# Filler projections: weights loaded and split half a group ahead, splits issued behind the newest probabilities' parts, in pieces of 512 columns

## The chip, the cores and the metric

The kernel runs on one core of one Trainium2 chip. The metric is the device time of one execution in microseconds (us); the time before is the median of three runs. The engines are TensorE (PE in the profile, its weight loads PEld), VectorE (DVE), ScalarE (ACT), GpSimd (POOL) and SyncE (SP), which here only issues DMAs. Each engine works through its own list of instructions in order; semaphores join the lists.

## The reference

One inference step of a layer with d_model 1024, for 256 context tokens and 1024 latent tokens. Both kinds of tokens go through the same normalised input, two token mixers side by side, a gated merge, one output projection, and a squared-ReLU MLP:

```python
h = rms_norm(x, norm_mix_w) * (1.0 + sc1) + sh1
z = h @ w_in                       # 1024 x 5376
hq, hf_f, hf_b, hi, hg, aq, ak, av, gl = jnp.split(z, _split_points(), axis=-1)
...                                # q, k normed, rotated; latent also sees 512 cached keys
o_a = block_attention(q, k_all, v_all)                      # 8 heads, 2 kv heads, 64 wide
o_h, s_final = hgrn_branch(hq, hf_f, hf_b, hi, hg, ...)     # scan in both directions
g = jax.nn.sigmoid(gl).reshape(b, l, 2, 1024)
merged = g[:, :, 0] * (o_h @ w_ho) + g[:, :, 1] * (o_a @ w_ao)
x = x + g1 * (merged @ w_out)
h = rms_norm(x, norm_ffn_w) * (1.0 + sc2) + sh2
x = x + g2 * (jnp.square(jax.nn.relu(h @ w_ff1)) @ w_ff2)
```

The shifts, scales and gates (sh1, sc1, g1, sh2, sc2, g2) are columns of silu(c) @ w_ada + b_ada, the adaLN product. All of it is float32. The 5376 columns of w_in are: hq, hf_f, hf_b, hi, hg with 512 each (for the scan), the queries, keys and values of the attention, and gl with 2048 (the merge gates).

## The kernel before

**Products.** A float32 product is made of three matmuls of a rounded type: each operand is split into a high part (rounded) and a low part (what is left), and high x high, high x low and low x high are added. The helper `split` does this to a piece of weights in SBUF: ACT copies it to the high part with rounding (L277), and DVE subtracts that from the raw piece to give the low part (L278). The matmuls of `mm3` are L308, L309 and L310.

**Stages.** The kernel goes through: normalisation and the projection of the attention's q, k, v (to about 150 us), the attention (to about 710 us), the scan of the HGRN branch (to about 1010 us), the merge and output projection, and the MLP. Attention and scan leave gaps on TensorE where a softmax or a recurrence isn't ready, so their matmuls are interleaved with those of projections that need nothing from them, the *filler*.

**The filler.** A group of the filler is 256 columns of w_in, applied to all 1280 tokens. During the attention run ten groups, five for each half of the scan's channels: hq, hf_f, hf_b as *channel groups* (`z_ch`: channels on the partitions, two halves of 128 columns after one another, 24 steps of three matmuls each), hi and hg as *token groups* (`z_tok`: tokens on the partitions, L325 to L327, 80 steps). During the scan run eight groups of gl, all channel groups. The class `Filler` advances such a generator by a given share of time between the matmuls of the attention or the scan. `with_ada` strings groups together and puts one block of 256 columns of the adaLN product behind each: a load of w_ada, 32 matmuls (L178), and a late part (a transposition L184 and a column sum `adas` on DVE, L186), which is called at the seventh step of the next group.

**The weights of a group.** `wraw` allots one of two buffers and issues the DMA of 1 MB (1024 x 256) on SP; the loads of w_in and w_ada take turns in them. `w_oc` (a half of a channel group) and `w_kh` (a half of a token group's rows) take two of six buffers `wsp`, a high and a low, and call `split` once for 1024 columns. All this stands in the program where the group, or its second half, begins.

**The attention.** A unit is one head and 256 queries. For the latent tokens its keys are three blocks of 512, and the unit goes through six *parts*: `trans` transposes two 128-key slices of the normalised probabilities `pexp` for both row blocks into one PSUM bank (L738), ACT takes the high part `pTh` of it (L741), DVE the low part `pTl` (L742), and `value` multiplies both with the values (L753 with `pTh`, L754 with `pTl`). Meanwhile the next unit's softmax runs: scores (L697) into three banks, maxima `mx` (DVE, L698), their negated maximum `ngm` (L702), three exponentials `pexp` for each row block (ACT, L708), the reciprocal sum `rs` (L711, L712), and the multiplication with it (L716), in turn on POOL and DVE.

**What sets the order.** TensorE's list is written out by the program (events of the units, merged by time, with filler between). The lists of ACT, DVE, POOL and SP are set by the framework's list scheduler: it simulates the program with costs of its own and issues on each engine, as buffers come free, what is ready, lower program order first. `tc.high_priority(offset=n)` makes it treat instructions as n earlier. Splits therefore go to the lists as soon as it believes the raw weights landed and the buffers free.

Of the kernel before, what the change touches and what calls it, by code (L numbers as in the profile page):

```python
# [44 lines left out]
def build(ctx, tc, I, O, C):  # L45
# [27 lines left out]
    def PS(tag, shape=(P, 512)):  # L73
        tag = "g" if tag == "p" else tag
        return ps.tile(list(shape), F32, tag=tag, name="ps_" + tag, bufs=PSB[tag])
# [30 lines left out]
    def f32(ap):  # L106
        return ap.bitcast(F32)
# [168 lines left out]
    def split(hi, lo, raw):  # L276
        s_.activation(hi, raw, AF.Copy)  # L277
        return v.tensor_tensor(lo, raw, f32(hi), op=ALU.subtract)  # L278
# [11 lines left out]
    def w_oc(raw, half, kcs=KC):  # L290

        hi, lo = wsp((P, kcs, P)), wsp((P, kcs, P))
        last_split[0] = split(hi, lo, raw[:, :, half * P:(half + 1) * P])
        return hi, lo

    def w_kh(raw, half):
        hi, lo = wsp((P, 4, 256)), wsp((P, 4, 256))
        split(hi, lo, raw[:, half * 4:half * 4 + 4, :])
        return hi, lo

    def mm3(out, wt, kcs, mov, first=True, last=True, mid=None):
# [27 lines left out]
                        consume(pr, po)  # L329
                    yield 0.327  # L330

    def z_ch(c0, consume, begun=None):

        raw, wt = begun or (wraw(I["w_in"], KC, c0), None)
        for half in range(2):
            if half or wt is None:
                wt = w_oc(raw, half)
            for t, (t0, n, cond) in enumerate(TT):
                po = PS("g")
                for k in range(KC):  # L340
                    mm3(po[:, 0:n], (wt[0][:, k:k + 1], wt[1][:, k:k + 1]), 1, hT[t][k:k + 1], k == 0, k == KC - 1)
                    if k == KC - 1:
                        consume(half, t, po[:, 0:n])
                    yield n * 0.00128

    def run(gen):
        for _ in gen:
# [313 lines left out]
    class Unit:  # L661
# [71 lines left out]
        def trans(self, p2):  # L733
            pt = PS("t", (P, 2, 256))
            for a in range(2):
                i, kg, b = self.kt[2 * p2 + a]
                for j in range(2):
                    pe.transpose(pt[:, a, j * P:(j + 1) * P], self.Ps[j][i][:, b * P:(b + 1) * P], ident)  # L738
            hi = S((P, 2, 256), F32R, name="pTh")
            lo = S((P, 2, 256), F32R, name="pTl")  # L740
            s_.activation(hi, pt, AF.Copy)  # L741
            v.tensor_tensor(lo, pt, f32(hi), op=ALU.subtract)  # L742
            self.pt[p2] = hi, lo

        def value(self, p2):
# [334 lines left out]
        return f  # L1080

    def zh(c):
        return (z_ch(HQ + 256 * c, hq_consume(c)), z_ch(HF + 256 * c, hf_consume(0, c)),
                z_ch(HF + 512 + 256 * c, hf_consume(1, c)), z_tok(HI + 256 * c, hi_consume(c)),
                z_tok(HG + 256 * c, hg_consume(c)))

    todo = []

    def with_ada(gens, b0):

        for i, gen in enumerate(gens):
            for j, x in enumerate(gen):
                if j == 6 and todo:
                    todo.pop()()
                yield x
            if b0 + i < 16:
                raw = wraw(I["w_ada"], KC, 2 * D + (b0 + i) * 256)
                ci = 16 + 2 * (b0 + i)
                todo.append(ada_cols(PS("g"), raw, ci))
                yield 1.8  # L1100
        if todo and b0:
            todo.pop()()
# [6 lines left out]
    R = S(name="R")  # L1109
    g_.memset(R, 0.0)  # L1110
    g_.memset(R.rearrange("p (c i) -> p c i", i=32)[:, :, 0:1], 1.0)
    raw = wraw(I["w_in"], KC, GL)
    with tc.high_priority(offset=600):
        begun = [(raw, w_oc(raw, 0))] + 7 * [None]
    fg = Filler(with_ada([z_ch(GL + 256 * c, gl_consume(c), begun[c]) for c in range(8)], 10), 194.0)
    hgrn(fg, fz.rest)
    fg.rest()
    close("sl")
# [708 lines left out]
```

## Time and profile before

| | |
|---|---|
| Time, median of 3 runs | 2056.11 us (2056.02 to 2057.93) |
| Time of the profiled execution | 2055.24 us |
| Its span, first to last instruction | 2053.1 us |
| Granted TensorE clock, mean | 0.998 |
| Busy in the span: PE, PEld, DVE, ACT, POOL | 2012.3, 1736.1, 1405.3, 938.5, 546.1 us |
| Splits of weights `wsp<-wraw`: ACT, DVE (all stages) | 109.7 us, 139.9 us (110 each) |
| High and low parts of probabilities `pTh` (ACT), `pTl` (DVE) | 118.4 us, 135.9 us (200 each) |

The profile is one execution. A row of a group of instructions names line, engine, operation, output<-input tile, shape and count. A row of the timeline gives start, duration and, in brackets, for how long the engine had been idle and which work of which engine ended that. TensorE is busy 98% of the span; its idle time in the stages of the attention and the scan is the small remainder in which the change acts.

### The profile page before, as it was taken

The page shows a single profiled execution, that of the slowest core. Times are in us where ns is not written, and L with a number is a line of the kernel's source. Part 1 is how long each engine was busy: PE and PEld are TensorE (multiplying, and loading weights), DVE is VectorE, ACT ScalarE, POOL GpSimd, SP SyncE. Part 2 cuts the span into 40 slices and gives each one's busy share as a digit, 9 for nine tenths or more (in the row PEclk, how much of TensorE's full clock was granted, in tenths as well). Part 3 has the DMA queues.
Part 4 walks back from the last instruction along what each step waited for, and adds up shares of the span by engine and source line. Part 5 has one row for each costly group of instructions (what it writes and reads, how often), then busy time and mean ns, then how long its engine had stood idle before and what let it go on. Part 6 is the DMA issues. An engine that isn't in the chain of part 4 may idle for free.

```text
span 2053.1 us, 33691 instructions
## 1 busy us (share of the span) xinstructions
PE 2012.3 (98%) x12470; PEld 1736.1 (85%) x12470; DVE 1405.3 (68%) x2655; ACT 938.5 (46%) x1906; POOL 546.1 (27%) x566
## 2 busy tenths in 40 slices
PE   6899999999999999999999999999999999999998
PEld 5798889988889988888888889998888888888886
DVE  4876776777776788779254634886666666577686
ACT  4735555555555423332321335655455544333443
POOL 1473333333332265545112101222122110000130
PEclk9999999999999999999999999999999999999999
DMA  9453220322211455455544533864444489455764
GB/s 309 150 187 97 78 77 27 108 86 78 78 45 65 132 175 167 153 173 159 196 138 149 180 113 116 259 186 151 157 147 157 145 292 361 148 159 176 232 238 142
DMA packets 220052, 317.38 MB, mean 155 GB/s; under 512 B 18504, under 2 KB 139168, under 8 KB 219888
## 3 DMA queue, kind: packets, MB, share of 16 engines
q1 hardware_dynamic: 207216, 275.05, 41.7%
q0 software_dynamic: 12672, 40.18, 5.5%
q8 instruction: 98, 1.61, 0.3%
q14 instruction: 66, 0.54, 0.1%
HBM read 229.43 MB, written 85.74 MB: 154 GB/s over the span
## 4 chain that ended last, share of the span: by engine, by line
PE 62%; DVE 2%; issue 1%; ACT 0%; DMA 0%; POOL 0%; POOLq 0%; ACTq 0%; DVEq 0%
PE ps_g L308 5%; PE ps_g L309 5%; PE ps_g L310 5%; PE ps_g L1614 2%; PE ps_g L1616 2%; PE ps_g L1615 2%; PE ps_s L1460 2%; PE ps_s L1461 2%; PE ps_s L1459 2%; PE ps_s L1614 2%; PE ps_s L1615 2%; PE ps_s L1616 2%; PE ps_t L1614 2%; PE ps_t L1615 2%; PE ps_t L1616 2%; PE ps_s L308 2%
## 5 line engine op out<-in xcount | busy, mean ns | idle before, releaser
L308 PE MATMUL ps_g<-hs,wsp 128*128 128x512 f32 (+1 forms) x896 | 322.2, 360 | 1.1 <-DVE adas L186 1.0
L310 PE MATMUL ps_g<-hs,wsp 128*128 128x512 f32 (+1 forms) x896 | 309.3, 345 | 0.0
L309 PE MATMUL ps_g<-hs,wsp 128*128 128x512 f32 (+1 forms) x896 | 309.1, 345 | 0.0
L716 POOL TENSOR_SCALAR pexp<-pexp,rs 128x512 f32<-128x512 f32 (+1 forms) x104 | 171.5, 1655 | 364.8 <-ACT pTh L741 210.6
L277 ACT ACTIVATE wsp<-wraw 128x1024 fp32r<-128x1024 f32 x110 | 109.7, 997 | 276.6 <-PE ps_g L309 82.8
L278 DVE TENSOR_TENSOR wsp<-wraw,wsp 128x1024 fp32r<-128x1024 f32 x110 | 139.9, 1272 | 114.8 <-ACT wsp L277 114.4
L308 PEld LDWEIGHTS ps_g<-hs,wsp 128*128 128x128 f32 x896 | 169.6, 189 | 22.3 <-issue 4.6
L310 PEld LDWEIGHTS ps_g<-hs,wsp 128*128 128x128 f32 x896 | 169.3, 189 | 21.5
L309 PEld LDWEIGHTS ps_g<-hs,wsp 128*128 128x128 f32 x896 | 169.9, 190 | 14.8
L741 ACT ACTIVATE pTh<-ps_t 128x512 fp32r<-128x512 f32 x200 | 118.4, 603 | 124.5 <-PE ps_t L738 124.4
L277 ACT ACTIVATE ah<-ar 128x640 fp32r<-128x640 f32 (+1 forms) x112 | 80.9, 723 | 185.1 <-PE ps_g L1615 102.3
L698 DVE TENSOR_REDUCE mx<-ps_s 128x1 f32<-128x512 f32 (+1 forms) x208 | 137.1, 663 | 37.7 <-PE ps_s L697 36.9
L708 ACT ACTIVATE pexp<-ps_s,ngm 128x512 f32<-128x512 f32 (+1 forms) x208 | 137.4, 670 | 43.7 <-DVE ngm L702 42.9
L278 DVE TENSOR_TENSOR ah<-ar,ah 128x640 fp32r<-128x640 f32 (+1 forms) x112 | 93.1, 832 | 77.2 <-ACT ah L277 76.1
L742 DVE TENSOR_TENSOR pTl<-ps_t,pTh 128x512 fp32r<-128x512 f32 x200 | 135.9, 681 | 14.1 <-ACT pTh L741 13.9
L697 PE MATMUL ps_s<-Kl,Ql 128*128 128x512 f32 (+1 forms) x416 | 130.7, 411 | 0.7 <-ACT pexp L708 0.7
L738 PE MATMUL ps_t<-ident,pexp 128*128 128x128 f32 x800 | 120.8, 273 | 3.3 <-DVE pTl L742 1.8
L325 PE MATMUL ps_g<-wsp,hs 128*128 128x256 f32 x400 | 115.9, 290 | 0.0
L327 PE MATMUL ps_g<-wsp,hs 128*128 128x256 f32 x400 | 112.9, 282 | 0.0
L326 PE MATMUL ps_g<-wsp,hs 128*128 128x256 f32 x400 | 112.5, 281 | 0.0
L754 PE MATMUL ps_g<-pTl,Vl 128*128 128x256 f32 x400 | 105.9, 287 | 4.0 <-DVE pTl L742 4.0
L738 PEld LDWEIGHTS ps_t<-ident,pexp 128*128 128x128 f32 x800 | 93.6, 140 | 14.1 <-issue 4.0
(421 smaller groups left out, 5395.2 us busy)
## 6 DMA issues: line engine op xcount, KB each, us to landing
ar<-AF SPq DMA_DIRECT2D x112, 320.0 KB, 3.2
wraw<-in_w_ff SPq DMA_DIRECT2D x32, 1024.0 KB, 6.1
wr<-in_w_ff SPq DMA_DIRECT2D x128, 256.0 KB, 4.4
wraw<-in_w_in SPq DMA_DIRECT2D x18, 1024.0 KB, 5.7
wraw<-in_w_ada SPq DMA_DIRECT2D x16, 1024.0 KB, 5.6
AF<-a POOLq DMA_DIRECT2D x48, 256.0 KB, 2.7
AF<-t POOLq DMA_DIRECT2D x48, 256.0 KB, 2.4
wa<-in_w_ada SPq DMA_DIRECT2D x32, 256.0 KB, 5.8
```

The lines of the kernel that those rows point to most:

```text
L277: s_.activation(hi, raw, AF.Copy)
L278: return v.tensor_tensor(lo, raw, f32(hi), op=ALU.subtract)
L308: pe.matmul(out, hi[:, k, :], mh, start=(first and k == 0), stop=False)
L309: pe.matmul(out, hi[:, k, :], ml, start=False, stop=False)
L310: pe.matmul(out, lo[:, k, :], mh, start=False, stop=(last and k == kcs - 1))
L697: pe.matmul(pq[:, 0:n], self.qh[:, q0:q0 + P], K[self.g][var][self.kts[i]], start=(var == 0), stop=(var == 1))
L698: v.tensor_reduce(self.mx[j][:, i:i + 1], pq[:, 0:n], axis=AX.X, op=ALU.max)
L708: s_.activation(e[:, 0:n], self.ps.pop((j, i))[:, 0:n], AF.Exp, bias=self.mx[j], accum_out=self.sm[j][:, i:i + 1])
L716: NORM[(i + j) % len(NORM)].tensor_scalar(x, x, self.rs[j], None, op0=ALU.mult)
L738: pe.transpose(pt[:, a, j * P:(j + 1) * P], self.Ps[j][i][:, b * P:(b + 1) * P], ident)
L742: v.tensor_tensor(lo, pt, f32(hi), op=ALU.subtract)
L1614: pe.matmul(bank, ph, wh, start=first and i == 0, stop=False, **more)
```

## The change

The two generators of a channel group become one for a half (`z_half`). A class `Group` holds a group's buffer and its split halves: `load` issues the load, `part(i)` splits half i, and `stages` yields what is to be multiplied. `with_ada` now calls these ahead: at half of a channel group's first half, its second half is split; at 5% of a group's last half (or of a token group's 80 steps) the load of the next group is issued in the program, and at 50% its first half is split, for a token group behind a channel group at 75% also the second.

While a split is issued it is ordered behind the newest `pTh` (on ACT) and the newest `pTl` (on DVE) that the program had made by then (`tc.issue_after` on both), which the attention leaves in `behind`. Behind the attention, `behind` still holds the last parts, so in the scan the rule holds nothing back.

Each split is cut into pieces of 512 columns, an ACT and a DVE instruction for each: `w_oc` in four of its eight slices at a time, `w_kh` in two of four. `w_oc` also serves the output projection later, with 8 splits of 1024 columns that become 16.

```diff
     def w_oc(raw, half, kcs=KC):
         hi, lo = wsp((P, kcs, P)), wsp((P, kcs, P))
-        last_split[0] = split(hi, lo, raw[:, :, half * P:(half + 1) * P])
+        for k in range(0, kcs, 4):
+            last_split[0] = split(hi[:, k:k + 4], lo[:, k:k + 4], raw[:, k:k + 4, half * P:(half + 1) * P])
         return hi, lo
     def w_kh(raw, half):
         hi, lo = wsp((P, 4, 256)), wsp((P, 4, 256))
-        split(hi, lo, raw[:, half * 4:half * 4 + 4, :])
+        for k in range(0, 4, 2):
+            split(hi[:, k:k + 2], lo[:, k:k + 2], raw[:, half * 4 + k:half * 4 + k + 2, :])
         return hi, lo
...
+    behind = [None, None]
+    class Group:
+        def __init__(self, c0, consume, tok):
+            self.c0, self.consume, self.tok = c0, consume, tok
+            self.raw, self.w = None, [None, None]
+        def load(self):
+            if self.raw is None:
+                self.raw = wraw(I["w_in"], KC, self.c0)
+        def part(self, i):
+            if self.w[i] is not None:
+                return
+            self.load()
+            with ExitStack() as after:
+                for x in behind:
+                    if x is not None:
+                        after.enter_context(tc.issue_after(x.ins))
+                self.w[i] = (w_kh if self.tok else w_oc)(self.raw, i)
+            if i == 1:
+                self.raw = None
+        def stages(self):
+            if self.tok:
+                self.part(0)
+                self.part(1)
+                w, self.w = self.w, [0, 0]
+                yield (0, 1), 80, z_tok(self.c0, self.consume, w)
+                return
+            for half in range(2):
+                self.part(half)
+                w, self.w[half] = self.w[half], 0
+                yield (half,), 24, z_half(w, half, self.consume)
+                del w
...
-            s_.activation(hi, pt, AF.Copy)
-            v.tensor_tensor(lo, pt, f32(hi), op=ALU.subtract)
+            behind[:] = s_.activation(hi, pt, AF.Copy), v.tensor_tensor(lo, pt, f32(hi), op=ALU.subtract)
...
-    def with_ada(gens, b0):
-        for i, gen in enumerate(gens):
-            for j, x in enumerate(gen):
-                if j == 6 and todo:
-                    todo.pop()()
-                yield x
+    def with_ada(groups, b0):
+        for i, grp in enumerate(groups):
+            nxt = groups[i + 1] if i + 1 < len(groups) else None
+            for need, n, gen in grp.stages():
+                if not grp.tok and need == (0,):
+                    jobs = [(0.5, lambda: grp.part(1))]
+                elif nxt:
+                    jobs = [(0.05, nxt.load), (0.5, lambda: nxt.part(0))]
+                    if nxt.tok and not grp.tok:
+                        jobs.append((0.75, lambda: nxt.part(1)))
+                else:
+                    jobs = []
+                for j, x in enumerate(gen):
+                    if 0 in need and j == 6 and todo:
+                        todo.pop()()
+                    while jobs and j >= jobs[0][0] * n:
+                        jobs.pop(0)[1]()
+                    yield x
...
-    raw = wraw(I["w_in"], KC, GL)
+    gls = [Group(GL + 256 * c, gl_consume(c), False) for c in range(8)]
     with tc.high_priority(offset=600):
-        begun = [(raw, w_oc(raw, 0))] + 7 * [None]
+        gls[0].part(0)
```

The lists of instructions show what the scheduler makes of it. TensorE's list of matmuls is the same in both kernels. On the other engines, at three places (in the changed kernel the line numbers are some 37 higher: `pTh` and `pTl` both stand at L778, `pexp` at L745, `mx` at L735, `ngm` at L739, `ze`, the evacuation of a projection, at L878 and L879, where it was L842 and L843).

The first place is DVE in a latent unit in the middle of the attention, the one that runs around 517 us. Before:

```order
L742 TENSOR_TENSOR pTl<-ps_t,pTh 128x512
L698 TENSOR_REDUCE mx<-ps_s 128x1
L742 TENSOR_TENSOR pTl<-ps_t,pTh 128x512
L698 TENSOR_REDUCE mx<-ps_s 128x1 x2
L742 TENSOR_TENSOR pTl<-ps_t,pTh 128x512
L702 TENSOR_REDUCE ngm<-mx 128x1
```

And now:

```order
L778 TENSOR_TENSOR pTl<-ps_t,pTh 128x512
L735 TENSOR_REDUCE mx<-ps_s 128x1
L278 TENSOR_TENSOR wsp<-wraw,wsp 128x512
L735 TENSOR_REDUCE mx<-ps_s 128x1
L278 TENSOR_TENSOR wsp<-wraw,wsp 128x512
L778 TENSOR_TENSOR pTl<-ps_t,pTh 128x512
L735 TENSOR_REDUCE mx<-ps_s 128x1
```

Two split pieces and one maximum have come between two `pTl`. The old split of 1024 columns stood one unit earlier, behind two of that unit's maxima (around 502 us).

The second place is ACT in the second latent unit, around 191 to 201 us. Before:

```order
L741 ACTIVATE pTh<-ps_t 128x512 x3
L708 ACTIVATE pexp,sm<-ps_s,ngm 128x512 x3
L741 ACTIVATE pTh<-ps_t 128x512
L842 ACTIVATE ze<-ps_g 128x512
```

And now:

```order
L778 ACTIVATE pTh<-ps_t 128x512 x2
L277 ACTIVATE wsp<-wraw 128x512 x2
L778 ACTIVATE pTh<-ps_t 128x512 x2
L745 ACTIVATE pexp,sm<-ps_s,ngm 128x512 x3
L878 ACTIVATE ze<-ps_g 128x512
```

Two split pieces have come in, and the unit's fifth `pTh` has moved ahead of the three exponentials of the next unit's second row block. On DVE the multiplication of those with `rs` has moved behind the last `pTl` of the unit with them.

The third place is DVE in the scan, around 737 us, ahead of the column sum `adas` of the adaLN product (`um`, `uq` and `ucp` belong to the scan). Before:

```order
L921 COPY um<-ucp 128x4x3
L922 TENSOR_TENSOR um<-ucp 128x4x2
L924 RECIPROCAL um<-ucp 128x4x4
L931 TENSOR_TENSOR uq<-uq,ucp 128x512
L907 TENSOR_TENSOR um<-um,ucp 128x4
L923 TENSOR_TENSOR um<-um,ucp 128x4
```

And now:

```order
L957 COPY um<-ucp 128x4x3
L958 TENSOR_TENSOR um<-ucp 128x4x2
L960 RECIPROCAL um<-ucp 128x4x4
L967 TENSOR_TENSOR uq<-uq,ucp 128x512
L278 TENSOR_TENSOR wsp<-wraw,wsp 128x512 x2
L943 TENSOR_TENSOR um<-um,ucp 128x4
L959 TENSOR_TENSOR um<-um,ucp 128x4
```

`adas` comes next in both lists; two split pieces have come ahead of it. The other lists differ in the same manner: the load of w_ada stands one store of `ze` earlier in SP's list, and the loads of w_in nearly where they stood.

More of the change, by code (lines that the diff above doesn't have):

```diff
@@ L330, in z_tok, with z_half @@
                     yield 0.327
[L332 to L344, printed above, removed]
+    def z_half(wt, half, consume):
+        for t, (t0, n, cond) in enumerate(TT):
+            po = PS("g")
+            for k in range(KC):
+                mm3(po[:, 0:n], (wt[0][:, k:k + 1], wt[1][:, k:k + 1]), 1, hT[t][k:k + 1], k == 0, k == KC - 1)
+                if k == KC - 1:
+                    consume(half, t, po[:, 0:n])
+                yield n * 0.00128
+    behind = [None, None]
[29 more added lines that the diff above has]
+                del w
     def run(gen):
@@ L1082, in zh @@
     def zh(c):
-        return (z_ch(HQ + 256 * c, hq_consume(c)), z_ch(HF + 256 * c, hf_consume(0, c)),
-                z_ch(HF + 512 + 256 * c, hf_consume(1, c)), z_tok(HI + 256 * c, hi_consume(c)),
-                z_tok(HG + 256 * c, hg_consume(c)))
+        return (Group(HQ + 256 * c, hq_consume(c), False), Group(HF + 256 * c, hf_consume(0, c), False),
+                Group(HF + 512 + 256 * c, hf_consume(1, c), False), Group(HI + 256 * c, hi_consume(c), True),
+                Group(HG + 256 * c, hg_consume(c), True))
     todo = []
-    def with_ada(gens, b0):
-        for i, gen in enumerate(gens):
-            for j, x in enumerate(gen):
-                if j == 6 and todo:
-                    todo.pop()()
-                yield x
+    def with_ada(groups, b0):
[16 more added lines that the diff above has]
+                    yield x
             if b0 + i < 16:
@@ L1111, in build @@
     g_.memset(R.rearrange("p (c i) -> p c i", i=32)[:, :, 0:1], 1.0)
-    raw = wraw(I["w_in"], KC, GL)
+    gls = [Group(GL + 256 * c, gl_consume(c), False) for c in range(8)]
     with tc.high_priority(offset=600):
-        begun = [(raw, w_oc(raw, 0))] + 7 * [None]
-    fg = Filler(with_ada([z_ch(GL + 256 * c, gl_consume(c), begun[c]) for c in range(8)], 10), 194.0)
+        gls[0].part(0)
+    fg = Filler(with_ada(gls, 10), 194.0)
     hgrn(fg, fz.rest)
```

## The prediction

> **What bounds the kernel now.** I read the busy times of the stretches first, then what TensorE waited for in them, then the splits' own rows, then the moments around single waits. In the stretches the columns are length, then busy time and count of PE, PEld, DVE, ACT and POOL, the granted clock, DMA share and GB/s.
>
> ```profile
> 150.00:710.00 560.00, 551.71 (x3982) 498.44 (x3981) 392.43 (x864) 313.10 (x738) 180.39 (x111) 1.00 0.24 79
> 710.00:1010.00 300.00, 298.81 (x2490) 255.54 (x2489) 232.61 (x542) 92.48 (x221) 149.20 (x157) 1.00 0.54 171
> ```
>
> The first row is the attention with the projections of ten groups between its matmuls, the second the scan with eight more groups. TensorE is busy 98.5% of the one and 99.6% of the other, at full clock; DVE stands at 392/560 = 70%, ACT at 56%. TensorE's list of instructions is the same in both kernels, so the only thing that can shrink is its idle time: 560 - 551.71 = 8.3 us, and 1.2 us in the scan. What ended that idle time in the attention (us in total, times, longest):
>
> ```profile
> PE ps_g L754 <- DVE pTl L742: 4.0, 10, 0.8
> PE ps_t L738 <- DVE pTl L742: 1.8, 3, 0.9
> PE ps_t L738 <- DVE pexp L716: 1.3, 3, 0.7
> PE ps_s L697 <- ACT pexp L708: 0.7, 2, 0.4
> ```
>
> Together 7.8 us in 18 waits, nearly all for work of DVE on the probabilities: the low part `pTl` or a normalised `pexp`. These matmuls are no wait for weights. The split comes in as what stands ahead of that work:
>
> ```profile
> 501.01 1.06 ACT L277 ACTIVATE wsp<-wraw 128x1024 fp32r<-128x1024 f32 x1 [1.73 <-DMA wraw<-in_w_in]
> ...
> 502.26 1.21 DVE L278 TENSOR_TENSOR wsp<-wraw,wsp 128x1024 fp32r<-128x1024 f32 x1
> ...
> 503.25 0.28 PE L753 MATMUL ps_g<-pTh,Vl 128*128 128x256 f32 x1
> 503.39 0.68 DVE L742 TENSOR_TENSOR pTl<-ps_t,pTh 128x512 fp32r<-128x512 f32 x1
> ...
> 504.12 0.39 PE L754 MATMUL ps_g<-pTl,Vl 128*128 128x256 f32 x1 [0.59 <-DVE pTl L742]
> ```
>
> (start, duration; in brackets the idle time before and what ended it.) ACT sat 1.73 us at the split's place until its load had landed, DVE then spent 1.21 us on the low part, and `pTl` behind it came 0.59 us late for L754. The idle figure understates the loss: from L753 to L754 there are 0.87 us here, and where nothing waits 0.13 (519.50 to 519.63, below), so 0.74 are lost, about 0.16 more than the bracket says.
>
> **The change, part by part.** *The size.* In the attention 20 splits of 1024 columns (12 of channel groups, 8 of token groups) become 40 of 512; all projections' 36 become 72, and 8 more of the output projection 16.
>
> ```profile
> L277 ACT ACTIVATE wsp<-wraw x110: 632/1060/1068, 105.1 to 1650.5; 128x1024 fp32r<-128x1024 f32 x94, 128x512 fp32r<-128x512 f32 x16
> L277 ACT ACTIVATE wsp<-wq x4: 615/676/720, 94.3 to 101.4; 128x512 fp32r<-128x512 f32 x4
>   DMA wraw<-in_w_in: 63.1, 17
> ...
> L278 DVE TENSOR_TENSOR wsp<-wq,wsp x4: 679/680/686, 98.6 to 104.8; 128x512 fp32r<-128x512 f32 x4
> L278 DVE TENSOR_TENSOR wsp<-wraw,wsp 128x1024 fp32r<-128x1024 f32 x17 | 20.7, 1220 | 6.1 <-ACT wsp L277 6.1
> ...
> wraw<-in_w_in SPq DMA_DIRECT2D x18, 1024.0 KB, 5.7
> ```
>
> (Shortest/median/longest ns; then DVE between 170 and 705 us, and the page's row of the loads, us to landing.) One split of 1024 is 1.06 us on ACT and 1.22 on DVE, two of 512 are 2 x 0.68 = 1.35 and 2 x 0.68 = 1.36: 0.29 and 0.14 us more a split at the most, less since neighbours overlap by some 0.08 (pitch 0.60). Over 44 splits that is up to 13 us of ACT and 6 of DVE, spread over 860 us at 70% DVE and 56% ACT or less. I cost it at nothing by itself; without that cover it would be those 6 to 13 us.
>
> *The wait at the head.* ACT spent 63.1 us in 17 waits on the loads of w_in. The load keeps nearly its place in SP's queue (SP carries the stores of z ahead of it, and the adaLN load goes one store earlier), but the splits come 0.45 of half a group after it, 560/10/2 x 0.45 = 12.6 us, against 5.7 us to landing. ACT will no longer wait there. Nothing of that is TensorE's time except through `pTh`, `pexp` and `pTl` queued behind, which are the stalls just counted; it is not a second gain.
>
> *Where the old splits go away.* Stalls that follow directly on a split, first to last, and the longest:
>
> ```profile
> 247.61 0.39 PE L754 MATMUL ps_g<-pTl,Vl 128*128 128x256 f32 x1 [0.16 <-DVE pTl L742]
> ...
> 567.20 0.39 PE L754 MATMUL ps_g<-pTl,Vl 128*128 128x256 f32 x1 [0.80 <-DVE pTl L742]
> ...
> 691.70 0.50 PE L697 MATMUL ps_s<-Kl,Ql 128*128 128x256 f32 x2 [0.30 <-ACT pexp L708]
> ```
>
> There are eight: 0.16 + 0.57 (377) + 0.29 (439) + 0.31 (441) + 0.59 (504) + 0.80 + 0.37 (636) + 0.30 = 3.4 us of idle, with 8 x 0.16 of pitch 4.7 us. Four more stand where the new order also has DVE or ACT do something else first:
>
> ```profile
> 192.30 0.63 PE L738 MATMUL ps_t<-ident,pexp 128*128 128x128 f32 x4 [0.26 <-DVE pTl L742]
> 231.72 0.39 PE L754 MATMUL ps_g<-pTl,Vl 128*128 128x256 f32 x1 [0.29 <-DVE pTl L742]
> 280.47 0.55 PE L738 MATMUL ps_t<-ident,pexp 128*128 128x128 f32 x3 [0.69 <-DVE pexp L716]
> 590.39 0.63 PE L738 MATMUL ps_t<-ident,pexp 128*128 128x128 f32 x4 [0.86 <-DVE pTl L742]
> ```
>
> 2.1 us, with pitch 2.7. Removed at best: 7.4 us. The ceiling, all 18 waits and the scan's, is 7.8 + 18 x 0.16 + 1.2 = about 12 us.
>
> *Where the new splits stand: (A) between two low parts.* Behind the newest `pTl` means ahead of the maxima and of the next `pTl`. At three places of the new DVE order (around 454, 517 and 549 us) it reads pTl, mx, split, mx, split, pTl, where it was pTl, mx, pTl, mx:
>
> ```profile
> 517.32 0.68 DVE L698 TENSOR_REDUCE mx<-ps_s 128x1 f32<-128x512 f32 x1
> 517.91 0.68 DVE L742 TENSOR_TENSOR pTl<-ps_t,pTh 128x512 fp32r<-128x512 f32 x1
> 518.51 0.68 DVE L698 TENSOR_REDUCE mx<-ps_s 128x1 f32<-128x512 f32 x1
> ...
> 519.50 0.28 PE L753 MATMUL ps_g<-pTh,Vl 128*128 128x256 f32 x1
> 519.63 0.28 PE L754 MATMUL ps_g<-pTl,Vl 128*128 128x256 f32 x1
> ```
>
> At a pitch of 0.60 the low part that began at 517.91 slips by two splits and one maximum to 519.7, ends near 520.4, and is wanted at 519.63: 0.8 us, three times 2.4. Bounds: 0 (ACT, ahead of DVE, has the probabilities so early that DVE runs ahead there) and 3 x 1.2.
>
> *(B) The second-last part of a unit goes ahead of the next unit's exponentials.* In nine units (five before 335 us, four after) the new ACT order has `pTh`, splits, `pTh`, and only then the three `pexp` of the second row block, where it had them ahead of that `pTh`; on DVE the normalisation falls behind the last `pTl`. One of them as it is now:
>
> ```profile
> 194.80 0.69 ACT L708 ACTIVATE pexp<-ps_s,ngm 128x512 f32<-128x512 f32 x1 [1.18 <-DVE ngm L702]
> 195.55 0.60 PE L738 MATMUL ps_t<-ident,pexp 128*128 128x128 f32 x4
> 197.34 1.32 DVE L716 TENSOR_SCALAR pexp<-pexp,rs 128x512 f32<-128x512 f32 x2
> 197.56 1.70 POOL L716 TENSOR_SCALAR pexp<-pexp,rs 128x512 f32<-128x512 f32 x1 [3.63 <-ACT pTh L741]
> 200.75 0.60 PE L738 MATMUL ps_t<-ident,pexp 128*128 128x128 f32 x4
> ```
>
> The transposes of 195.55 end at 196.15; `pTh` takes 0.6, so the exponentials start near 196.75 instead of 194.80, and the normalisations, 2.54 us behind their start and behind one more `pTl`, near 199.9; two take 1.3 us on DVE, one 1.7 on POOL, so they end about 201.2 to 201.6, and the next unit's first transposes want them at 200.75. I take 0.9 us here. The other eight, worked the same way from their slack: 0.65, 0.6, 0.5, 0.8, 1.2, 1.0, 0.25 and nothing; 5.9 in all. Bounds: 0, since the exponentials may find `ngm` so late that the order changes nothing, and 1.2 for each, 10.8. The nearest row that shows such an order at work is the 280.47 above: 0.69 of idle, 0.85 lost, and I keep the middle for that.
>
> *(C) Scores.* Near 619 us two splits stand ahead of three exponentials:
>
> ```profile
> 617.58 0.69 ACT L708 ACTIVATE pexp<-ps_s,ngm 128x512 f32<-128x512 f32 x1
> 619.41 1.17 PE L697 MATMUL ps_s<-Kl,Ql 128*128 128x512 f32 x4
> ```
>
> They slip by two splits and one `pTh`, 1.8 us, to 619.4, and give back their three banks of scores that much later: 1.0 us at L697, between 0 and 1.8.
>
> *(D) The scan.* Its one wait is the adaLN column sum on DVE, and two splits now stand directly ahead of that sum:
>
> ```profile
> 738.13 0.39 PE L308 MATMUL ps_g<-hs,wsp 128*128 128x256 f32 x1 [1.05 <-DVE adas L186]
> 741.18 1.86 DVE L278 TENSOR_TENSOR wsp<-wraw,wsp 128x1024 fp32r<-128x1024 f32 x1
> ```
>
> Two halves there are 1.2 us at the attention's pitch, up to 2.3 at the scan's slower rate. I take 1.3 more; behind the sum L308 to L310 wait, the whole group. Below nothing is possible too: the splits elsewhere in the scan no longer jump ahead of the scan's own work, but 1.2 us in all is what can be won.
>
> The sum: -7.4 + 2.4 + 5.9 + 1.0 + 1.3 = **+3.2 us**. Against the profiled execution, 2055.24, that is 2058.4; the median of the runs, 2056.11, is 0.87 above it, so **2059.3 us**.
>
> A rule that would add to it: the Trainium skill, "SBUF — State Buffer", section "SBUF: two separate sides", says that VectorE and GpSimd share one port pair, which a VectorE operation with two SBUF inputs and a GpSimd operation that reads SBUF lock against one another for a whole instruction. A split's low part has two such inputs, and normalisations run on POOL just where the new splits stand. The attention's rows don't show it:
>
> ```profile
> 564.05 1.83 POOL L716 TENSOR_SCALAR pexp<-pexp,rs 128x512 f32<-128x512 f32 x1 [3.81 <-DVE rs L712]
> 565.34 1.21 DVE L278 TENSOR_TENSOR wsp<-wraw,wsp 128x1024 fp32r<-128x1024 f32 x1
> ```
>
> The split began 0.54 us before POOL's end and took no longer than the others. By the skill's rule it would have waited these 0.54 us, and (A) would be 3 x 0.5 dearer, the sum +4.7; by the row it stays. In the scan the 1.86 us beside POOL's work go the rule's way, and the 2.3 of (D) is its upper end without it.
>
> **The rivals.** *Clean gain.* Every stall named as removable goes and (A) to (D) cost nothing: 2056.11 - 7.4 = 2048.7, or 2051.4 if only the eight behind splits go. For it: DVE has 30% free, ACT no longer stands at a load, halves can be fitted into shorter gaps. Against it: the new places are fixed by position behind a part and not by a gap; 517.91 shows a place without one.
>
> *Slower: normalisations behind the last part.* (B) alone, at its upper end of 10.8, with (D) at 2.3: -7.4 + 10.8 + 2.4 + 1.0 + 2.3 = +9.1, 2065.2 us. It decides over everything else from 6.8 us on, 0.75 per unit, for then the sum passes +4.1. For it: 280.47. Against: the row at 194.80 shows ACT waiting 1.18 us for `ngm`, so part of the slip is there already.
>
> *The stall moves with the split.* A low part is wanted about 1.2 us after its high part whatever stands between, so forty halves delay as many parts as twenty wholes did, elsewhere: eight stalls again, only 2.7 us gone and about as much come in anew; 2056 us. For it: the count of DVE's work is the same. Against: (B), which is no matter of size.
>
> **How the numbers follow.** Forecast (+0 to +6 around +3.2): 0.47; moved stalls: 0.20; clean gain: 0.17; the slower rival: 0.16. A measurement of this kernel tells about 0.2%, 4.1 us, from no change. Faster by more: the clean gain, 0.17. Slower by more: the slower rival and the part of the forecast above +4.1, 0.16 + 0.13 = 0.29. Within: 0.54. The range goes from the nearer end of the clean gain, 2051, to just above the slower rival, 2066; the forecast's own is 2056 to 2062. Beyond it lie the farther half of the clean gain and the unknown ends of (C) and (D), under 0.2.
>
> **What would show it.** In the new profile, ACT's waits on the w_in loads (63.1 us) should be near nothing, the count of 128x512 splits up by 88 and their DVE time about 0.68 each. The L754 waits behind 377, 504 and 567 us should be gone, and new ones stand near 456, 520 and 551 us (A); the L738 waits on `pexp` should grow from 3 to about 10 (B), with 0.5 to 0.9 us each; L697 should wait near 620 (C), and L308 about 2.3 us instead of 1.05 near 738 us (D). If the attention's PE idle is below 5 us the forecast is wrong to the fast side; if L738 on `pexp` alone exceeds 8 us, to the slow side; if TensorE is held by a load of w_in, the landing was not as early as I read it.

## The result

| | before | changed |
|---|---|---|
| Median of 20 runs each | 2055.49 us (2053.15 to 2057.93) | 2059.95 us (2058.58 to 2062.26) |
| Ratio, 95% interval | | 1.0022 (1.0015 to 1.0028) |
| Profiled execution's span | 2053.1 us | 2057.1 us |

The changed kernel is slower by 0.22%, 4.5 us between the medians, just above what the prediction called no change (0.2%). The forecast was 2059.3 us. The number was met, but not by its own sum: the attention came out better than forecast and the scan worse, and the two misses cancelled, which is luck.

The same stretches of the changed kernel, attention and scan (length; busy time and count of PE, PEld, DVE, ACT and POOL; granted clock, DMA share, GB/s):

```profile
150.00:710.00 560.00, 551.71 (x3991) 499.06 (x3990) 394.23 (x882) 313.90 (x755) 179.36 (x111) 1.00 0.24 79
710.00:1010.00 300.00, 296.05 (x2465) 253.28 (x2465) 234.66 (x556) 91.72 (x234) 150.59 (x157) 0.99 0.53 167
```

TensorE is as busy in the attention as it was, 551.71 us. In the scan it stands at 296.05 instead of 298.81, and the granted clock of that stretch shows 0.99. What TensorE waited for between 170 and 715 us, in the changed kernel:

```profile
PE ps_t L775 <- DVE pexp L753: 4.3, 9, 0.7
PE ps_g L790 <- DVE pTl L778: 2.3, 4, 0.7
PE ps_s L734 <- ACT pexp L745: 1.0, 2, 0.5
PE ps_t L775 <- DVE pTl L778: 0.4, 1, 0.4
```

L775 are the transposes (before L738), L790 the products with `pTl` (L754), L734 the scores (L697). The waits on low parts fell from 4.0 and 1.8 us to 2.3 and 0.4; those of the transposes on normalised probabilities rose from 1.3 to 4.3. The sum is 8.0 us against 7.8. And between 705 and 1015 us there is one wait:

```profile
PE ps_g L310 <- DVE adas L186: 4.0, 1, 4.0
```

It was 1.0. Since both kernels have the same 12,470 matmuls in the same order, each can be set against its counterpart, and the difference of their start times (from each span's start) shows where time is lost and gained. From this, for the profiled executions:

| stretch (times of the kernel before) | changed minus before |
|---|---|
| 160 to 710 us, attention | -0.45 us |
| 710 to 745 us, the column sum in the scan | +4.40 us |
| 745 to 1010 us, rest of the scan | -0.59 us |
| 1010 to 2040 us | +0.48 us |

The steps of this difference in the attention fall on the predicted places. Gone, in us at the times of the kernel before: 0.42 (192), 0.45 (232), 0.32 (248), 0.86 (280), 0.73 (377), 0.47 (441), 0.75 (504), 0.96 (567), 1.02 (590), 0.61 (636), 0.54 (692), 7.1 in all, and 1.7 more at five places that had not been named. New: 0.82 at each of 456, 520 and 551; 0.81 (201), 0.51 (233), 0.53 (264), 0.45 (296), 0.49 (344), 0.70 (375), 0.91 (407), 0.42 (439), 4.8 in all, at transposes; 0.76 (619), and at two more score matmuls 0.73 (301) and 0.28 (587). That is 9.0 against 8.8; another -0.7 us lies in steps below 0.18 us.

**(A), two pieces between two low parts.** DVE and the matmul that waits, around 520 us in the changed kernel:

```profile
518.22 0.67 DVE L735 TENSOR_REDUCE mx<-ps_s 128x1 f32<-128x512 f32 x1
518.81 0.68 DVE L278 TENSOR_TENSOR wsp<-wraw,wsp 128x512 fp32r<-128x512 f32 x1
519.41 0.68 DVE L735 TENSOR_REDUCE mx<-ps_s 128x1 f32<-128x512 f32 x1
520.01 0.68 DVE L278 TENSOR_TENSOR wsp<-wraw,wsp 128x512 fp32r<-128x512 f32 x1
...
520.61 0.68 DVE L778 TENSOR_TENSOR pTl<-ps_t,pTh 128x512 fp32r<-128x512 f32 x1
...
521.35 0.39 PE L790 MATMUL ps_g<-pTl,Vl 128*128 128x256 f32 x1 [0.66 <-DVE pTl L778]
```

Four operations at a pitch of 0.60 stand between the `pTl` before (517.62) and the next; L790 shows 0.66 of idle time, and 0.82 is lost.

**(B), normalisations behind the last part.** The unit around 191 to 201 us:

```profile
195.84 0.60 ACT L778 ACTIVATE pTh<-ps_t 128x512 fp32r<-128x512 f32 x1 [2.56 <-PE ps_t L775]
196.34 0.68 ACT L745 ACTIVATE pexp<-ps_s,ngm 128x512 f32<-128x512 f32 x1
...
199.75 0.53 DVE L879 TENSOR_SCALAR ze<-ze,fc,fc 128x512 f32<-128x512 f32 x1
...
200.20 0.68 DVE L778 TENSOR_TENSOR pTl<-ps_t,pTh 128x512 fp32r<-128x512 f32 x1
...
200.80 1.22 DVE L753 TENSOR_SCALAR pexp<-pexp,rs 128x512 f32<-128x512 f32 x2
201.33 0.55 PE L775 MATMUL ps_t<-ident,pexp 128*128 128x128 f32 x3 [0.65 <-DVE pexp L753]
```

The exponentials start behind the fifth `pTh`, at 196.34 (194.80 before, although the transposes ahead of it, at 195.20, are 0.35 us earlier now), DVE normalises behind the last `pTl` at 200.80 (197.34 before), and the transposes of the next unit wait.

**(D), the scan.** ACT, DVE, POOL and TensorE around 740 us:

```profile
737.43 2.13 DVE L278 TENSOR_TENSOR wsp<-wraw,wsp 128x512 fp32r<-128x512 f32 x2
737.59 2.88 POOL L949 TENSOR_TENSOR uw<-uq,um 128x512 f32<-128x512 f32 x2 [2.50 <-DVE uq L967]
739.49 1.00 DVE L943 TENSOR_TENSOR um<-um,ucp 128x4 f32<-128x4 f32 x1
...
740.49 0.15 DVE L186 TENSOR_REDUCE adas<-ps_g 128x4 f32<-128x8 f32 x1
...
740.69 0.58 PE L310 MATMUL ps_g<-hs,wsp 128*128 128x256 f32 x1 [3.95 <-DVE adas L186]
741.07 0.41 PE L311 MATMUL ps_g<-hs,wsp 128*128 128x256 f32 x1
741.28 0.41 PE L312 MATMUL ps_g<-hs,wsp 128*128 128x256 f32 x1
```

In the kernel before, DVE and POOL at this place:

```profile
737.78 0.15 DVE L907 TENSOR_TENSOR um<-um,ucp 128x4 f32<-128x4 f32 x1
737.92 0.15 DVE L186 TENSOR_REDUCE adas<-ps_g 128x4 f32<-128x8 f32 x1
737.94 2.06 POOL L913 TENSOR_TENSOR uw<-uq,um 128x512 f32<-128x512 f32 x2 [2.50 <-DVE um L907]
738.00 1.01 DVE L907 TENSOR_TENSOR um<-um,ucp 128x4 f32<-128x4 f32 x1
```

The two pieces took 2.13 us instead of 1.2, and the four-column product L943 (L907 before) behind them 1.00 instead of the 0.15 it had before, both beside POOL's work. In the kernel before that product and `adas` had been started by the time POOL began, at 737.94; the next such product, at 738.00, already stood beside POOL and took 1.01. Now POOL begins at 737.59, while the pieces are still on DVE. `adas` came at 740.49 instead of 737.92, and the wait was 3.95 instead of 1.05. Then TensorE went on at half speed: a matmul of 256 columns every 0.21 us, where it was every 0.12. The stretches' clock, in the column before the DMA share:

```profile
737.00:740.60 3.60, 0.00 (x0) 0.00 (x0) 3.60 (x7) 0.77 (x2) 3.01 (x3) 0.99 1.11 347
740.60:742.00 1.40, 1.31 (x6) 1.31 (x6) 1.40 (x4) 0.00 (x0) 1.10 (x1) 0.50 0.72 274
742.00:744.00 2.00, 2.00 (x34) 1.43 (x33) 1.97 (x8) 0.00 (x0) 0.00 (x0) 0.51 0.03 12
744.00:746.00 2.00, 2.00 (x20) 1.92 (x17) 2.00 (x3) 0.00 (x0) 1.90 (x1) 1.00 0.14 41
```

So of the +4.40, 2.9 us are the longer wait and 1.5 us the half clock from about 740.7 to 744.0 us.

### The profile page after: what moved, and what is told of

Read it like the earlier page. It is cut to its first block, busy times and chain, and to the rows that moved or that the text cites. A ratio compares the mean times of both kernels' runs of the same rounds, so it can differ in the third digit from the quotient of the medians.

```text
span 2057.1 us, 33840 instructions
## 1 busy us (share of the span) xinstructions
PE 2013.7 (98%) x12470; PEld 1737.5 (84%) x12470; DVE 1412.8 (69%) x2731; ACT 942.7 (46%) x1982; POOL 547.1 (27%) x566
## 4 chain that ended last, share of the span: by engine, by line
PE 85%; DVE 6%; ACT 2%; issue 1%; POOL 1%; DMA 1%; POOLq 0%; SPq 0%; DVEq 0%; ACTq 0%
PE ps_g L310 7%; PE ps_g L312 7%; PE ps_g L311 7%; PE ps_s L734 4%; PE ps_t L775 4%; PE ps_g L1664 2%; PE ps_g L1662 2%; PE ps_g L1663 2%; PE ps_s L1507 2%; PE ps_s L1508 2%; PE ps_s L1509 2%; PE ps_g L790 2%; PE ps_g L789 2%; PE ps_s L1662 2%; PE ps_s L1663 2%; PE ps_s L1664 2%
## 5 line engine op out<-in xcount | busy, mean ns | idle before, releaser
L277 ACT ACTIVATE wsp<-wraw 128x512 fp32r<-128x512 f32 (+1 forms) x186 | 116.8, 669 | 228.7 <-PE ps_g L311 90.9
L278 DVE TENSOR_TENSOR wsp<-wraw,wsp 128x512 fp32r<-128x512 f32 (+1 forms) x186 | 148.1, 819 | 100.6 <-ACT wsp L277 100.2
L778 ACT ACTIVATE pTh<-ps_t 128x512 fp32r<-128x512 f32 x200 | 119.2, 603 | 138.2 <-PE ps_t L775 137.8
L735 DVE TENSOR_REDUCE mx<-ps_s 128x1 f32<-128x512 f32 (+1 forms) x208 | 137.3, 664 | 39.3 <-PE ps_s L734 38.4
L745 ACT ACTIVATE pexp<-ps_s,ngm 128x512 f32<-128x512 f32 (+1 forms) x208 | 137.3, 669 | 35.5 <-DVE ngm L739 34.7
L778 DVE TENSOR_TENSOR pTl<-ps_t,pTh 128x512 fp32r<-128x512 f32 x200 | 136.2, 681 | 15.1 <-ACT pTh L778 14.9
L734 PE MATMUL ps_s<-Kl,Ql 128*128 128x512 f32 (+1 forms) x416 | 130.9, 411 | 1.1 <-ACT pexp L745 1.0
L775 PE MATMUL ps_t<-ident,pexp 128*128 128x128 f32 x800 | 122.2, 274 | 4.8 <-DVE pexp L753 4.3
L775 PEld LDWEIGHTS ps_t<-ident,pexp 128*128 128x128 f32 x800 | 93.6, 140 | 16.6 <-DVE pexp L753 6.9
L790 PE MATMUL ps_g<-pTl,Vl 128*128 128x256 f32 x400 | 105.3, 286 | 2.4 <-DVE pTl L778 2.3
```

Of the source, the lines that this page charges most:

```text
L734: pe.matmul(pq[:, 0:n], self.qh[:, q0:q0 + P], K[self.g][var][self.kts[i]], start=(var == 0), stop=(var == 1))
L735: v.tensor_reduce(self.mx[j][:, i:i + 1], pq[:, 0:n], axis=AX.X, op=ALU.max)
L745: s_.activation(e[:, 0:n], self.ps.pop((j, i))[:, 0:n], AF.Exp, bias=self.mx[j], accum_out=self.sm[j][:, i:i + 1])
L778: behind[:] = s_.activation(hi, pt, AF.Copy), v.tensor_tensor(lo, pt, f32(hi), op=ALU.subtract)
L790: pe.matmul(pv[:, 0:256], V[self.g][kg][:, b, :], lo[:, a, :], start=False, stop=(k == last))
```

## The experiments

The theory after the result: a split costs where its pieces stand in a row ahead of something that TensorE wants within about 1 us. In the attention the new places cost as much as the old ones, and what the medians show is the scan's one wait. The rivals: the loss is the attention's; the size of the pieces is the cause; the order behind the parts is the cause. Shifts of matched matmuls are given as in the table above, against the kernel before, attention from 160 to 710 us, and the column sum from 710 to 745. They are those of one execution each. In the first 160 us the profiled executions start the attention 0.4 us earlier to 3.2 us later than that of the kernel before, so medians need not follow the shifts to the microsecond.

### The splits behind the column sum

```diff
-            v.tensor_reduce(x.rearrange(...), pt.rearrange(...)[...], axis=AX.X, op=ALU.add)   # adas
+            behind[2] = v.tensor_reduce(x.rearrange(...), pt.rearrange(...)[...], axis=AX.X, op=ALU.add)
```

(`behind` has a third entry for it, and `part` orders each split behind all three.)

> The changed kernel; the only edit orders the splits on DVE also behind the newest adaLN column sum, so that in the scan the two split pieces near 737 us stand behind that sum; the attention's lists stay as they are. Theory (in the scan, the two pieces ahead of the column sum cost 4.4 us: 2.9 of longer wait and 1.5 of matmuls at half clock after it; the attention's gains and losses nearly cancel): 2059.95 - 4.4 = 2055.6 us, the wait at the column sum back to about 1 us and no granted clock of 0.5 near 741 us. Rival (the loss sits in the attention, and the scan's wait is taken back by a later slack): 2059 to 2060 us.

Measured: 2055.97 us, the kernel before beside it 2055.85, ratio 0.9998 (0.9989 to 1.0007). Attention -0.47, column sum -1.13 us. Between 715 and 1010 us the view of TensorE's waits is empty, and TensorE is busy 295.00 of these 295 us; the pieces, now behind the sum, take longer still and hold nobody up:

```profile
738.79 0.15 DVE L186 TENSOR_REDUCE adas<-ps_g 128x4 f32<-128x8 f32 x1
738.87 2.99 DVE L278 TENSOR_TENSOR wsp<-wraw,wsp 128x512 fp32r<-128x512 f32 x2
```

The whole loss of the change sits at this one place: with it gone, the median is where it was before. (The shifts in attention and scan add up to -2.2 us; the medians show no such gain, though the interval just reaches it.) The theory holds, and the rival (the attention) falls. The wait even went below the 1.05 us of before: there, a split of 1.21 us (728.10 in that trace) stood ahead of the scan's chain that leads to the sum, and here none does. That this is the reason is read from the two lists and was not tried by itself.

### Whole splits at the same places

```diff
-        for k in range(0, kcs, 4):
-            last_split[0] = split(hi[:, k:k + 4], lo[:, k:k + 4], raw[:, k:k + 4, half * P:(half + 1) * P])
+        last_split[0] = split(hi, lo, raw[:, :, half * P:(half + 1) * P])
```

and the same in `w_kh`.

> The changed kernel with whole splits of 1024 columns, which stand in the lists at the very places of the pairs of 512. Theory (place decides, not size: two pieces take 1.2 us of DVE in a row as one does): the 0.8 us stalls at the low parts near 456, 520 and 552 us stay, the scan's wait stays above 3 us, 2059 to 2061 us. Rival (the small pieces' fixed cost, up to 0.14 us on DVE and 0.29 on ACT for each of 44 splits, is what costs): 2054 to 2056 us.

Measured: 2059.21 us, ratio 1.0012 (1.0003 to 1.0022). Attention -1.03, column sum +3.53 us. The waits are those of the change:

```profile
PE ps_t L773 <- DVE pexp L751: 4.2, 9, 0.7
PE ps_g L788 <- DVE pTl L776: 2.1, 4, 0.6
PE ps_s L732 <- ACT pexp L743: 0.9, 2, 0.4
PE ps_t L773 <- DVE pTl L776: 0.4, 1, 0.4
```

and in the scan

```profile
PE ps_g L308 <- DVE adas L186: 3.0, 1, 3.0
```

Size is not the cause: whole splits at the same places lose 3.4 us where the pieces lose 4.5. The place is. The half clock came here too, behind 3.0 us of waiting.

### The kernel before with pieces of 512

The same cut, in the kernel before, and nothing else.

> The kernel before with its splits cut into pieces of 512 columns, and nothing else. Theory (size changes little): stalls behind splits as before, within 1.5 us of it, 2054 to 2057 us. Rival (each cut costs its extra 0.14 us of DVE and 0.29 of ACT on the path): 2058 to 2062 us.

Measured: 2056.40 us against 2055.85, ratio 1.0006 (0.9996 to 1.0016); attention +0.85, column sum 0.00. As the theory said: the pieces' extra time on DVE and ACT is hidden, to within a microsecond.

### No order behind the parts

```diff
-            behind[:] = s_.activation(hi, pt, AF.Copy), v.tensor_tensor(lo, pt, f32(hi), op=ALU.subtract)
+            s_.activation(hi, pt, AF.Copy)
+            v.tensor_tensor(lo, pt, f32(hi), op=ALU.subtract)
```

> The changed kernel without the order behind the newest parts; loads and splits are still traced half a group ahead, pieces of 512. DVE then takes a split about two parts earlier, as soon as the load landed. Theory (half a group ahead alone gives nothing; a split costs where it lands): the stalls at the three low parts go, others of 0.3 to 0.9 us come as in the kernel before, the scan's wait stays at 3 to 4 us (two pieces still stand ahead of the column sum): 2058 to 2061 us. Rival (the order behind the parts causes the attention's new stalls, and the lead alone would be a gain): attention 5 us or more faster, 2053 to 2055 us.

Measured: 2063.03 us, ratio 1.0031 (1.0019 to 1.0044); attention +1.29, column sum +5.37 us. It was worse than either theory said, above the 2058 to 2061 of the first. The waits moved as expected (transposes on `pexp` 4.4 us in seven, on `pTl` 1.9 in three, L791 on `pTl` 0.8 in three), and in the scan TensorE waited 3.9 us for the sum, as in the change. But the half clock lasted 6.8 us in this execution, from 743.5 to 750.3, instead of 3.4, and that is the column sum's further 1.0 us. Half a group's lead by itself is no gain, and the order behind the parts is not the cause of the loss.

### The order of the exponentials

(B) says that the transposes wait because the exponentials stand behind the fifth high part. So that order was put back:

```diff
-(-5.4, -4.9, -4.4, -2.4, -1.9, -1.4)      # when the six exponentials of a unit are issued in the program
+(-5.4, -4.9, -4.4, -2.4, -2.3, -2.2)
...
+            with ExitStack() as after:
+                if p2 == 4 and expd[0]:        # expd[0]: the newest exponential
+                    after.enter_context(tc.issue_after(expd[0].ins))
+                h = s_.activation(hi, pt, AF.Copy)
```

> The changed kernel, splits where it has them; the exponentials of a unit's second row block come earlier in the program and the fifth high part of the unit before is ordered behind them on ACT, in every latent unit. Theory (the new waits of the transposes are the exponentials behind the fifth part): the nine waits of 4.3 us at the transposes on the normalised probabilities fall to four or fewer and under 2 us, the attention 2.5 to 4 us shorter than in the change, the scan unchanged: 2056 to 2057.5 us. Rival (the exponentials wait for the maxima in either order, and the fifth high part is now held up with them): as much comes back as waits at L753 and L754 or stays at the transposes: 2059 to 2061 us.

Measured: 2064.07 us, ratio 1.0045 (1.0028 to 1.0061); attention +3.22, column sum +4.43 us. What TensorE waited for in the attention:

```profile
PE ps_g L794 <- DVE pTl L782: 8.6, 11, 1.3
PE ps_t L775 <- DVE pexp L753: 1.2, 3, 0.7
PE ps_s L734 <- ACT pexp L745: 0.5, 1, 0.5
PE ps_t L775 <- DVE pTl L782: 0.4, 1, 0.4
```

Both expectations came true in part, and the time missed the ranges of both. The waits on `pexp` fell from 4.3 us in nine to 1.2 in three, so the order of the exponentials is indeed what makes the transposes wait. But the fifth high part, now held behind the exponentials, and the low part behind it came late in turn: 8.6 us at L794 instead of 2.3. The rival was right about the direction and said too little: the loss over the change is 4 us. Near 345 us, where a stall of 0.49 us at the transposes went, one of 1.39 us came at L794:

```profile
342.10 1.09 ACT L781 ACTIVATE pTh<-ps_t 128x512 fp32r<-128x512 f32 x2
...
343.56 1.22 DVE L753 TENSOR_SCALAR pexp<-pexp,rs 128x512 f32<-128x512 f32 x2
344.70 0.67 DVE L782 TENSOR_TENSOR pTl<-ps_t,pTh 128x512 fp32r<-128x512 f32 x1
...
345.43 0.39 PE L794 MATMUL ps_g<-pTl,Vl 128*128 128x256 f32 x1 [1.23 <-DVE pTl L782]
```

So putting the order back does not mend (B). The edit reaches every latent unit: five of the new stalls at L794 (295, 343, 374, 407 and 437 us) stand in units where a stall at the transposes went, and one more, of 1.40 us near 564 us, in a unit where the change had none. The reading from these rows is that DVE, with two pieces of a split ahead of the maxima, is about as late as those two pieces are long at the end of such a unit, and that the order decides whether the normalisation or the low part pays; that is argued, not shown by a run. The order that the change has is the cheaper one.

### The pieces apart

If two pieces in a row are the trouble, one at a time should fit. `part` issues one piece per call, each behind the newest part of its own moment, and the splits also stand behind the column sum:

```diff
-                    jobs = [(0.5, lambda: grp.part(1))]
+                    jobs = [(0.5, lambda: grp.part(1, 1)), (0.7, lambda: grp.part(1))]
...
-                    jobs = [(0.05, nxt.load), (0.5, lambda: nxt.part(0))]
-                    if nxt.tok and not grp.tok:
-                        jobs.append((0.75, lambda: nxt.part(1)))
+                    jobs = [(0.05, nxt.load)]
+                    if nxt.tok and not grp.tok:
+                        jobs += [(0.4, lambda: nxt.part(0, 1)), (0.55, lambda: nxt.part(0)),
+                                 (0.7, lambda: nxt.part(1, 1)), (0.85, lambda: nxt.part(1))]
+                    else:
+                        jobs += [(0.5, lambda: nxt.part(0, 1)), (0.7, lambda: nxt.part(0))]
```

> The changed kernel with the scan's splits behind the column sum, as in the run before, and with the two pieces of a split issued apart from one another: each behind the newest part of its own, some two or three parts after the first. Theory (a stall comes where two pieces in a row, 1.2 us, exceed the slack of about 1 us; one piece fits): the waits at the low parts near 456, 520 and 552 us fall from 0.7 to at most 0.3 us, four units instead of nine have their exponentials behind the fifth part; the attention 4 to 7 us shorter than before, the scan 1 us: 2049 to 2052 us. Rival (DVE's work is what counts, wherever it stands): attention as before, 2054 to 2056 us.

Measured: 2051.18 us against 2055.32, ratio 0.9981 (0.9972 to 0.9991): faster than both kernels. Attention -3.29, column sum -1.14 us. Against the run with the splits behind the column sum, from which this one differs in the spread alone, the attention is 2.8 us shorter. Its gain over the kernel before is a little below the 4 us expected; the waits (170 to 715 us) fell to 5.1 us in all:

```profile
PE ps_t L778 <- DVE pexp L756: 2.5, 6, 0.7
PE ps_t L778 <- DVE pTl L781: 1.3, 2, 0.7
PE ps_g L793 <- DVE pTl L781: 1.3, 4, 0.4
```

At the three places of (A) the loss is 0.22 us each instead of 0.82, and DVE around the middle one shows why: one piece less stands between the two `pTl`.

```profile
515.48 0.68 DVE L781 TENSOR_TENSOR pTl<-ps_t,pTh 128x512 fp32r<-128x512 f32 x1
516.08 0.67 DVE L738 TENSOR_REDUCE mx<-ps_s 128x1 f32<-128x512 f32 x1
516.68 0.68 DVE L278 TENSOR_TENSOR wsp<-wraw,wsp 128x512 fp32r<-128x512 f32 x1
517.28 0.68 DVE L738 TENSOR_REDUCE mx<-ps_s 128x1 f32<-128x512 f32 x1
517.88 0.68 DVE L781 TENSOR_TENSOR pTl<-ps_t,pTh 128x512 fp32r<-128x512 f32 x1
```

Two other arrangements of single pieces asked whether that hung on the places hit: at 40 and 60% of a half, and at 35 and 80%.

> The spread pieces at other places: the first at 40% of a half and the second at 60% (token groups at 35, 50, 65, 80%) instead of 50 and 70 (40, 55, 70, 85). Theory (single pieces fit nearly everywhere): 2049 to 2053 us. Rival (the gain hangs on the places hit): 2054 to 2057 us.

> The spread pieces farther apart, at 35 and 80% of a half (token groups at 30, 50, 70, 90%). Theory (single pieces fit nearly everywhere): 2049 to 2053 us. Rival (the gain hangs on the places hit): 2054 to 2057 us.

Measured: 2051.64 us, ratio 0.9982 (0.9973 to 0.9991), attention -4.08; and 2051.83 us, ratio 0.9983 (0.9974 to 0.9993), attention -3.39. In these three arrangements the places hardly matter. And the same spread without the order behind the parts, where the scheduler's list has the pieces mostly in twos again, in places four that start within 2.4 us:

> The spread pieces without the order behind the newest parts. In the lists the pieces run together again, two and four in a row on DVE, about when the load lands. Theory (it is the order behind the parts that keeps the pieces apart, and pieces in a row stall): the attention as before or up to 3 us longer, the scan 1 us shorter, 2054 to 2058 us. Rival (the lead of half a group and the spread in the program suffice): 2050 to 2052 us.

Measured: 2057.07 us, ratio 1.0010 (1.0001 to 1.0020), attention +1.19, column sum -1.11. The profiled execution has one more wait, 2.9 us at about 1376 us, with the half clock behind it; no other run here shows over 0.5 us there, and the attention's figure does not hang on it. Without the order the spread in the program is undone, and with it the gain: -3.29 becomes +1.19.

Last, the spread pieces with the order of the exponentials:

> The spread pieces and the order of the exponentials together. Theory: both gains add where they concern different units, the attention 6 to 9 us shorter than before, the scan 1 us: 2047 to 2050 us. Rival (once the pieces are spread the order of the exponentials brings nothing more): the same as with the spread pieces alone within 1 us.

Measured: 2055.11 us, ratio 0.9998 (0.9988 to 1.0007), attention -0.79. Both expectations missed: the order that costs 3.7 us of attention with paired pieces (3.22 + 0.45) costs 2.5 with single ones (waits on the low part 5.2 us in nine).

## Why the prediction was right, point by point

- **The bound** (TensorE's idle time for DVE's work on the probabilities, no wait for weights) was right; the changed profile's waits are of the same four kinds, and in attention and scan the kernels here moved hardly anything but them and the column sum.
- **The wait at the head** of ACT for w_in's loads fell from 63.1 us in 17 to 12.5 in two, and no gain came with it, as said.
- **The size** costing nothing was right, by two runs. Its count was wrong: 76 splits were cut, not 44, since `w_oc` also serves the MLP, with 32 splits (40 of the 76 come behind the scan). DVE had 5.0 us more of `wsp<-wraw` between 1010 and 1900 us (82.2 against 77.2), and TensorE was as busy there as before, 889.04 against 889.06 us.
- **Removed, 7.4 us:** 7.1 at eleven of the twelve named places. The twelfth, at 439, did not go and even grew by 0.42: its unit is one of those of (B), so the sum had counted it on both sides. 1.7 us more went at places not named.
- **(A), 2.4 us:** three times 0.82, 2.5, at the three places. **(C), 1.0:** 0.76.
- **(B), 5.9 us:** 4.8 at eight transposes, where nine units had been counted. The places and the mechanism held, the single sizes were off by up to half a microsecond (0.9 forecast and 0.81 measured at the first), and the run that put the order back showed that it could not be had for nothing, which the prediction did not see.
- **(D), 1.3 us:** this is the term that was mis-sized. It came to 4.4. The upper end of its bounds was 2.3, the scan's rate for two pieces. The wait grew by 2.9: 2.06 for the two pieces, within that bound, and 0.85 for the four-column product behind them, which the sum had put at nothing, although the row at 738.00 of the kernel before shows that product at 1.01 beside POOL's work. Another 1.5 us came from the clock that dropped behind a wait of that length. In the attention and the scan of the kernel before no wait was over 1.05 us; its one early stretch at half clock, from 25.3 to 28.7 us, had not been drawn on. The -0.59 us in the rest of the scan are not a part of (D): they stand at the same two places, 926 and 947 us, in every kernel here, also in the kernel before with pieces of 512, whose column sum did not move.
- **The sum:** attention +1.9 forecast, -0.45 measured; scan +1.3 forecast, +3.8 measured. The errors are +2.4 and -2.5, and that they cancel is luck. In the attention 1.7 us more went at places not named and (B) cost 1.1 less, while two score matmuls that nobody had forecast (301 and 587 us) cost 1.0. The forecast of 2059.3 was right for the kernel as a whole and wrong for each half of it; it also stood on a median of 2056.11, and against the 2055.49 of 20 runs the change is +4.5 us, not +3.2.
- **The rivals:** the clean gain did not come, since the new places cost as much as the old. The slower rival needed 10.8 us at (B) and found 4.8. The stall that moves with the split comes nearest to the attention's result, but not for its reason: single pieces do not only move the stalls, they bring the attention's waits from 7.8 us down to 5.1.
- **The Trainium skill's rule** on the shared port ("SBUF — State Buffer", section "SBUF: two separate sides") was set aside for the attention by the 565 us row. (A) came out at 0.82 each, but it is no test of the rule: the changed kernel's trace has no work of POOL beside any of its six pieces. Beside normalisations on POOL, 11 of 13 pieces took 0.68 or 0.69 us, as by that row, the other two 0.93 and 1.11. In the scan the rows go the rule's way, and there it reached one instruction further than the prediction had counted.

## What to carry to other kernels

Work that is interleaved on an engine with 30% of its time free still has to go in pieces smaller than the slack at each place. At (A) that slack was about 1 us, and a maximum stood in it too: one piece of 0.6 us cost 0.22 us there, two cost 0.82. Cutting a block in two without keeping the halves apart did nothing. When a scheduler orders engines by its own estimate, the anchor can be needed as much as the cut: here it is what kept the pieces apart. And list, for every engine on which moved work lands, the small things behind it that a bank or a matmul waits for; one four-column reduction carried this whole change's loss.

## What the runs showed of the hardware

**The clock after a wait.** In the changed kernel the granted clock was 0.50 from 740.6 to 744.0 us, behind a TensorE wait of 3.95 us; behind the 1.05 us wait of the kernel before at the same place it was 1.00 (the figure before the DMA share):

```profile
738.10:740.00 1.90, 1.87 (x38) 1.58 (x38) 1.90 (x4) 1.90 (x4) 1.90 (x2) 1.00 1.14 331
```

From the attention on, the half clock came behind every TensorE wait of 2.9 us and more: in the experiments for 3.4 us behind 3.0 us (whole splits), behind 3.9 us (the order of the exponentials) and behind the 2.9 us near 1376 us, and for 6.8 us behind 3.9 us (no order behind the parts). At the column sum it cost 1.5 us on top of the wait where it lasted 3.4 us, and 2.5 us where it lasted 6.8. It began between 1.3 us before TensorE went on and 1.3 us after, so a single execution does not fix what such a wait costs. The Trainium skill, "TensorE: Matmul & The Clock Gate", section "What's actually happening", says that about 3.4 us of idling take the array to half its clock, until it has again been busy for about as long. The trace agrees in the length of the stretch, 3.4 us and once twice that; the waits of 2.9 and 3.0 us lie under the figure and had it too.

**DVE beside POOL.** The splits of 512 columns on DVE, in the changed kernel from 170 to 705 us and from 705 to 1010:

```profile
L278 DVE TENSOR_TENSOR wsp<-wraw,wsp 128x512 fp32r<-128x512 f32 x34 | 22.9, 701 | 0.0
```

```profile
L278 DVE TENSOR_TENSOR wsp<-wraw,wsp 128x512 fp32r<-128x512 f32 x32 | 26.2, 845 | 8.3 <-ACT wsp L277 8.3
```

In the attention POOL runs one-input operations (the normalisations), and most splits beside them keep their 0.68 us. In the scan it runs two-input operations, and splits beside them take up to 1.7 us; two pieces took 2.99 us in the run with the column sum first. That the second input is what makes the difference was not tried, and it can't be all: in that same run three pieces beside a two-input operation of POOL on four columns, near 981 us, kept their 0.68 us.
